# A two-layer decoder trunk on one core: the shift of each sublayer as two columns of the high activations, split once a layer, and another rule of waiting in the planner

## Chip, core and metric

The kernel runs on one core of a Trainium2 chip. The metric is device time in microseconds (us) of one execution; the lower the better. Before the change three runs took 947.19, 947.73 and 947.96 us, median 947.73. An execution under the profiler took 947.46 us. Its trace spans 945.7 us from the first to the last instruction, at a mean granted TensorE clock of 0.998.

## What is computed

A trunk of two layers, 256 tokens of width 1024, all in float32. Each layer has three sublayers: a SwiGLU feed-forward network (FFN), a token mixer (stick-breaking attention in layer 0, a gated linear recurrence in layer 1) and a second FFN. A conditioning vector `c` gives each sublayer a shift, a scale and a gate:

```python
mod = (c_act @ mod_w[layer] + mod_b[layer]).reshape(B, N_SUB, 3, D_MODEL)
...
h = rmsnorm(x, g) * (1 + scale[:, None, :]) + shift[:, None, :]
...
x = x + MACARON_W * g * swiglu(h, ffn_w_gu[layer, 0], ffn_w_down[layer, 0])
...
x = x + g * y
...
return rmsnorm(x, final_norm_g)
```

`D_FF` is 2816, the recurrent width 1280, and the weights fill some 249 MB, each read once.

## The kernel before

**Layout.** Activations are held transposed: `x` is eight tiles, one for each 128 of the 1024 features, of 128 partitions by 256 tokens. Weights stand still in TensorE, 128 x 128 at a time, and 256 token columns move through. A line number L610 is line 610 of the kernel.

**Three passes.** A float32 product is made of three float32r products. A number is split into a high part, rounded to float32r, and a low part, the rest. `group` (L598) issues for each piece of weights: high weights by high activations, high weights by low activations, low weights by high activations (`seq`, L607; the pass numbers are 0, 1, 2). Weights are split as they come in (`load`, L559): ACT copies the high part (`wh`, L581), DVE subtracts (`wl`, L584).

**A border** is the change from one sublayer to the next; five of the six sublayers have one ahead of them (generations (0,1), (0,2), (1,0), (1,1), (1,2)). The norm's factor for a token isn't known until all eight tiles of `x` are done, so the first two weight tiles behind a border (`NFIRST`) are computed from the activations without it. `scaled` (L712) makes for each chunk `d` a tile `hi` and a tile `lo` out of the ring `hx`, each of 258 columns (`TX`): 256 with `x` times the scale, and two with the shift, split anew for each chunk (L719, L720), the same value in both. `up_first` (L839) multiplies these 258 columns in all three passes, 2 weight tiles by 2 halves by 8 chunks. Its `evict` (L854) takes from PSUM the 256 columns times the factor `q` (tile `tr`, L857) and the product of the shift column (tile `bc`, L856). Meanwhile `norm` (L741) makes the normed activations, in `norm_chunk` (L725), for every weight tile that follows, with 256 columns.

**The rest of a sublayer.** `up` (L824) multiplies the normed `hx` by the weight tiles. `down` (L756) multiplies the result, which lies split in a high and a low half in the arena (`arenar`), by the down weights: for an FFN 22 chunks by 8 outputs by 3 passes, 528 matmuls; for the recurrent block 10 x 8 x 3, 240; for attention 8 x 8 x 3, 192. `residual` (L775) adds to `x` and calls `scaled` for the next border.

**Modulation.** Between the weight tiles, `mod_tile` (L636) computes shift, scale and gate of later sublayers on DVE from rows of `mod_w`, and `mod_final` (L648) adds the bias; for a shift (`w == 0`) that is L657.

**Places in SBUF.** Tiles get their addresses in the order of allocation, each rounded up to 32 bytes; the arena comes behind all of them. Three pads of odd sizes stand between: `HXPAD` 112, `HKPAD` 16 and `ARPAD` 56 columns of 4 bytes. With them the byte addresses in a partition are: `wh` from 43136, `wl` from 72704 (their views begin 0 or 128 bytes in, in turn, so that each begins at 128 modulo 256), `hx` from 102720 in steps of 1280, `hk` at 128384 and 129408, the arena at 168000. `hk` (L746, `other_copy`) holds a second copy of the first normed chunk; it is used for the first six matmuls of some weight tiles (`kick` in `up`), hx for the others. In a few places `kick_op` (L833) puts a short matmul of zeros ahead.

**The order of work** is planned by the program as it is built. `schedule` (L190) lists every operation with a cost, a due time (`prio`, from the TensorE order) and its dependences, and simulates the engines. For ACT and DVE, `wait_for` (L252) decides whether an operation that could start at `t` is held back because one that is due earlier will be ready at `g`, before the first would end; then a shorter one is taken or the engine idles. SP issues the weight loads in the planned order.

Of the kernel before, what the change touches and what calls it, by code (L numbers as in the profile page):

```python
# [8 lines left out]
F32R = mybir.dt.float32r  # L9
BF16 = mybir.dt.bfloat16  # L10
AF = mybir.ActivationFunctionType
ALU = mybir.AluOpType
PSUM = bass.MemoryType.PSUM

P = 128
T = 256
TX = T + 2
D = 1024
KD = D // P
# [111 lines left out]
class Program:  # L131
# [58 lines left out]
    def schedule(self):  # L190
# [23 lines left out]
        for o in reversed(ops):  # L214
            p = o.nominal if o.nominal is not None else self.pe + 1e5
            for s, data in o.succ:
                p = min(p, s.prio - o.cost - self.lag(o, s, data))
            for s, held in o.soft:
                p = min(p, s.prio - (o.cost + 100.0 if held else 0.0))
# [32 lines left out]
        def wait_for(e, t, o):  # L252

            q = queue[e]
            while head[e] < len(q) and q[head[e]].start is not None:
                head[e] += 1
            n, i = 0, head[e]
            slack = o.prio + late - t
            while n < LOOK and i < len(q):
                u = q[i]  # L260
                i += 1
                if u.start is not None:
                    continue
                n += 1
                if u is o or u.prio >= o.prio:
                    break
                g = guess(u, 3)
                if g is None or g >= t + o.cost or g <= t:
                    continue
                if u.prio + late - g < o.cost and u.prio + late - g < slack - MARGIN:  # L270
                    return g
            return None
# [17 lines left out]
        while len(order) < len(ops):  # L290
            best, again = None, False
            for e, c in cand.items():
                ok = []
                for o in c:
                    t = possible(o)
# [6 lines left out]
                for t, o in ok:  # L302
                    if t > t0:
                        continue
                    p = o.prio
# [4 lines left out]
                if e in queue:  # L310
                    g = wait_for(e, pick[2], pick[3])
# [15 lines left out]
            t, _, o = best  # L327
            cand[o.eng].remove(o)
            if o.eng == "ACT":
                if t - busy >= TABLE_NS and (gap is None or t - busy > gap[0]):  # L330
                    gap = (t - busy, o)
                if o.table is not None:
                    if o.table != table:
                        if gap is None:
                            t, gap = busy + TABLE_NS, (0.0, o)
# [15 lines left out]
            for b in o.bufs:  # L351
                b.uses -= 1
                if b.uses == 0 and b.space is not None:
# [3 lines left out]
                    t = o.end + 120.0 if b.hist else o.end  # L357
# [38 lines left out]
def c_dve(n):  # L396
    return 68.0 + 1.042 * n
# [11 lines left out]
def trunk(ctx, tc, first_in, cb, par, modw, gu, wdn, qk, wv, wo, win, wri, wout, out):  # L409
    at_ = {}  # L410
    for *key, n in first_order():
        o = sum(P * q.shape[1] for q in at_.values())
        at_[tuple(key)] = first_in[o : o + P * n].rearrange("(p n) -> p n", n=n)
    nc = tc.nc
    act, dve, pe, pool, sp = nc.scalar, nc.vector, nc.tensor, nc.gpsimd, nc.sync
    ctx.enter_context(tc.manual_schedule())
    pr = Program()
# [4 lines left out]
    def f32(ap):  # L422
        return ap.bitcast(F32)
# [74 lines left out]
    def fixed(name, cols, dt=F32):  # L498
        return const.tile([P, cols], dt, tag=name, name=name)
# [27 lines left out]
    mraw, mfin = {}, {}  # L527
# [5 lines left out]
    def col(off, n=1):  # L533
        return pars()[:, off : off + n]

    for l in range(2):
        for q in range(3):
            for w in range(3):
                mraw[l, q, w] = Buf(ap=fixed(f"mr{l}{q}{w}", KD))
                mfin[l, q, w] = Buf(ap=fixed(f"mf{l}{q}{w}", KD))  # L540
    gbias = Buf(ap=fixed("gbias", KD))
    fixed("pad1", ARPAD)


# [6 lines left out]
    def A(o, i, f, n, r, w, table=None, psum=False, ptr=0, after=(), **kw):  # L551
        def fn():
            act.activation(o(), i(), f, **{k: (v() if callable(v) else v) for k, v in kw.items()})  # L553
        return pr.op("ACT", c_act(n, psum, ptr), fn, r, w, after, table)

    def V(fn, n, r, w, cost=None, ptr=0):
        return pr.op("DVE", cost or c_dve(n) + 62.0 * ptr, fn, r, w)

    def load(src, n, name, chain=None, sizes=None, plain=0, homes=(), behind=(), kind=Buf):  # L559

# [30 lines left out]
    class Acc:  # L591
# [3 lines left out]
            self.b = Buf(banks, name=name)  # L595
            self.started = False

        def group(self, part, o, w, wc, xs, xc, stop, parts=(None,), passes=(0, 1, 2)):  # L598

            b = self.b  # L600
            start = not self.started
            self.started = True
            wh, wl = w
            xh, xl = xs

            def fn():
                seq = ((wh, xh), (wh, xl), (wl, xh))  # L607
                for n, i in enumerate(passes):
                    u, v = seq[i]
                    pe.matmul(o(b()), wc(u()), xc(v()), start=start and n == 0, stop=stop and n == len(passes) - 1,  # L610
                              skip_group_check=True)

            n = xs_n[0]
            ws = [wh] * (passes != (2,)) + [wl] * (2 in passes)
            rd = ws + [(t, q) for t in [xh] * (passes != (1,)) + [xl] * (1 in passes) for q in parts]
            if not start:
                rd.append((b, "start"))
            wr = [(b, part)] + ([(b, "start")] if start else [])
            return pr.op("PE", c_mm(n, len(passes)), fn, rd, wr)
# [8 lines left out]
        pr.op("PE", c_mm(n, 4), lambda: pe.matmul(o(b()), wc(w()), xc(x32()), start=start, stop=stop, skip_group_check=True),  # L628
              [w, x32] + ([] if start else [(b, "start")]), [(b, part)] + ([(b, "start")] if start else []))

    def group(acc, part, o, w, wc, xs, xc, n, stop, parts=(None,), passes=(0, 1, 2)):
        xs_n[0] = n
        return acc.group(part, o, w, wc, xs, xc, stop, parts, passes)


    def mod_tile(l, s, w, t, after=(), lat=None, rate=RATE, home=None, behind=()):  # L636
# [11 lines left out]
    def mod_final(l, s, w, t0=0, n=KD):  # L648
        m, f = mraw[l, s, w], mfin[l, s, w]
        b = OFF_MB + (l * 9 + s * 3 + w) * KD + t0  # L650
        rr = [(m, t) for t in range(t0, t0 + n)]
        ww = [(f, t) for t in range(t0, t0 + n)]
        pp = [(pars, 0)] if l == s == 0 else [pars]
        mi = lambda: m()[:, t0 : t0 + n]
        fo = lambda: f()[:, t0 : t0 + n]
        if w == 0:
            V(lambda: dve.tensor_tensor(fo(), mi(), col(b, n), ALU.add), n, rr + pp, ww)  # L657
            return
        V(lambda: dve.tensor_tensor(mi(), mi(), col(b, n), ALU.add), n, rr + pp, rr)
        if w == 1:  # L660
            g = OFF_NG + (l * 3 + s) * KD + t0
            V(lambda: dve.scalar_tensor_tensor(fo(), mi(), 1.0, col(g, n), ALU.add, ALU.mult), n, rr + pp, ww)
        else:
            wt = MAC if s != 1 else 1.0
            V(lambda: dve.tensor_scalar(fo(), mi(), 1.0, wt, ALU.add, ALU.mult), n, rr, ww)


    ssq, hcur, gcur, hkick = {}, {}, {}, {}

    def add_square(gen, d):  # L670
        if d == 0:
# [39 lines left out]

    def scaled(gen, d):  # L712

        gs, sh = mfin[gen + (1,)], mfin[gen + (0,)]
        hi, lo = Buf(hxr), Buf(hxr)
        gcur.setdefault(gen, []).append((hi, lo))
        c = slice(d, d + 1)
        shc = lambda: sh()[:, c].to_broadcast([P, 2])
        A(lambda: hi()[:, T:], shc, AF.Copy, 2, [(sh, d)], [(hi, 1)])  # L719
        V(lambda: dve.tensor_tensor(lo()[:, T:], shc(), f32(hi()[:, T:]), ALU.subtract), 2, [(sh, d), (hi, 1)], [(lo, 1)])  # L720
        A(lambda: hi()[:, :T], x[d], AF.Copy, T, [x[d], (gs, d)], [(hi, 0)], ptr=1, scale=lambda: gs()[:, c])
        V(lambda: dve.scalar_tensor_tensor(lo()[:, :T], x[d](), gs()[:, c], f32(hi()[:, :T]), ALU.mult, ALU.subtract), T,
          [x[d], (gs, d), (hi, 0)], [(lo, 0)], ptr=1)

    def norm_chunk(gen, d, q, whole=False):  # L725
        gs, sh = mfin[gen + (1,)], mfin[gen + (0,)]
        hp, hi, lo = Buf(hpr), Buf(hxr), Buf(hxr)
        hcur.setdefault(gen, []).append((hi, lo))
        c = slice(d, d + 1)
        V(lambda: dve.scalar_tensor_tensor(hp(), x[d](), gs()[:, c], q(), ALU.mult, ALU.mult), T,  # L730
          [x[d], (gs, d), q] + [(sh, d)] * whole, [hp], ptr=1)
        h = None
        if whole:
            h = Buf(hpr)
            V(lambda: dve.tensor_scalar(h(), hp(), sh()[:, c], None, ALU.add), T, [hp, (sh, d)], [h], ptr=1)
        A(lambda: hi()[:, :T], hp, AF.Identity, T, [hp, (sh, d)], [hi], ptr=1, bias=lambda: sh()[:, c])
        V(lambda: dve.scalar_tensor_tensor(lo()[:, :T], hp(), sh()[:, c], f32(hi()[:, :T]), ALU.add, ALU.subtract), T,
          [hp, (sh, d), hi], [lo], ptr=1)
        return h

    def norm(gen, q):  # L741
# [97 lines left out]
    def up_first(gen, ws, scale=(1.0, 1.0)):  # L839


        gx = gcur.pop(gen)
        accs = {}
        for i, w in enumerate(ws):
            accs[i] = [Acc(f"first_{gen}_{i}_{g}") for g in range(2)]
            for k in range(KD):
                if (i, k) == ((0, 6) if gen == (0, 1) else (1, 0)):
                    q = rstd(gen)
                for g in range(2):
                    c0 = (k % 4) * 256 + g * P  # L850
                    group(accs[i][g], 0, lambda b: b[:, :TX], w[k // 4], lambda u, c0=c0: u[:, c0 : c0 + P], gx[k],
                          lambda v: v, TX, k == KD - 1, parts=(0, 1))

        def evict(i, g):  # L854
            b, t, c = accs[i][g].b, Buf(tr), Buf(bcr)
            V(lambda: dve.tensor_scalar(c()[:, :1], b()[:, T : T + 1], scale[g], None, ALU.mult), 1, [b], [c])  # L856
            V(lambda: dve.scalar_tensor_tensor(t(), b()[:, :T], scale[g], q(), ALU.mult, ALU.mult), T, [b, q], [t])  # L857
            return t, c, lambda: c()[:, :1]

        norm(gen, q)  # L860
        for i in range(len(ws)):
            yield [evict(i, g) for g in range(2)]
# [693 lines left out]
```

## Time and profile before

| | |
|---|---|
| runs, median (lowest to highest) | 947.73 us (947.19 to 947.96) |
| the profiled execution | 947.46 us |
| its span | 945.7 us |
| TensorE matmuls (PE), weight loads (PEld) | 8078 of each |
| VectorE (DVE) instructions | 1279 |
| ScalarE (ACT) instructions | 914 |
| read from HBM | 248.92 MB, 264 GB/s over the span |

How to read the profile's rows: a row of the timeline or of the chain begins with the start and the length in us. In a row of groups stand line, engine, operation, out<-in by the program's tile names, partitions x elements and type, the count behind `x`, then the busy time in us and the mean duration of one in ns, then the engine's idle time before them. Matmuls overlap, so the mean duration of one isn't the spacing; that comes from the starts. A row of windows gives the stretch, its length, and then for PE, PEld, DVE, ACT (and POOL) the busy us and the count.

### The profile page before, as it was taken

Reading aid. Unit: us, or ns where it says so; the run is one execution under the profiler, and the core shown is the slowest. Engines: PE = TensorE matmul, PEld = TensorE weight load, DVE = VectorE, ACT = ScalarE, POOL = GpSimd, SP = SyncE. Lnnn points to the kernel's source line nnn. Section 1 sums busy time; section 2 is a strip of 40 time slices with the busy share of each in tenths; the row PEclk is TensorE's granted clock in tenths of the full one; section 3 lists DMA queues with packets and bytes.
Section 4 is the critical chain, followed back from the end, with each engine's and each line's share of the span. In section 5 each row is a group of like instructions: output and inputs, shape, how many; then the busy total and the mean of one; then the engine's idle time right before and its main releaser. Section 6 shows DMA issues by size and latency. Waiting matters only on the chain.

```text
span 945.7 us, 19610 instructions
## 1 busy us (share of the span) xinstructions
PE 934.8 (99%) x8078; PEld 924.2 (98%) x8078; DVE 781.6 (83%) x1279; ACT 559.3 (59%) x914; POOL 2.1 (0%) x14
## 2 busy tenths in 40 slices
PE   8999999999999999999999999999999999999996
PEld 6999999999999999999999999999999999999996
DVE  7999888899987989888799998866999997555443
ACT  5785553488785754454367554544789675554343
POOL 0000000000000000000000000000000000000000
PEclk9999999999999999999999999999999999999999
DMA  9989989948833699889967999885253646555421
GB/s 362 404 332 368 340 333 361 364 170 320 294 133 130 269 337 359 319 313 359 348 250 275 346 348 353 327 321 223 90 198 116 223 189 244 192 186 211 170 104 45
DMA packets 48332, 251.25 MB, mean 266 GB/s; under 512 B 5361, under 2 KB 5745, under 8 KB 28530
## 3 DMA queue, kind: packets, MB, share of 16 engines
q1 hardware_dynamic: 47952, 249.59, 70.2%
q8 instruction: 63, 1.03, 0.4%
q10 hardware_dynamic: 290, 0.40, 0.1%
q14 instruction: 27, 0.22, 0.1%
HBM read 248.92 MB, written 1.05 MB: 264 GB/s over the span
## 4 chain that ended last, share of the span: by engine, by line
PE 97%; DVE 2%; DMA 1%; ACT 0%; issue 0%; SPq 0%; DVEq 0%
PE bank L610 90%; PE bank L1041 2%; PE bank L1274 1%; PE bank L916 1%; DMA arenar<-in_first_in 1%; PE bank L1107 1%; PE bank L1168 1%; DVE wl L584 1%; PE bank L1144 1%; DVE arenar L644 0%; DVE x L1386 0%; PE bank L1147 0%; DVE arenaf L1358 0%; PE bank L703 0%; DVE arenaf L1345 0%
## 5 line engine op out<-in xcount | busy, mean ns | idle before, releaser
L610 PE MATMUL bank<-hx,wh 128*128 128x256 f32 (+1 forms) x3264 | 560.4, 277 | 0.0
L581 ACT ACTIVATE wh<-raw 128x1024 fp32r<-128x1024 f32 (+1 forms) x330 | 335.3, 1037 | 281.9 <-PE bank L610 199.0
L610 PEld LDWEIGHTS bank<-hx,wh 128*128 128x128 f32 x3264 | 492.7, 188 | 0.0
L584 DVE TENSOR_TENSOR wl<-raw,wh 128x1024 fp32r<-128x1024 f32 (+1 forms) x330 | 386.6, 1196 | 118.5 <-ACT wh L581 114.8
L610 PE MATMUL bank<-hx,wl 128*128 128x256 f32 (+1 forms) x1640 | 452.7, 277 | 0.0
L610 PEld LDWEIGHTS bank<-hx,wl 128*128 128x128 f32 x1640 | 308.4, 188 | 0.0
L610 PE MATMUL bank<-arenar,wh 128*128 128x256 f32 x1696 | 289.4, 276 | 0.0
L610 PEld LDWEIGHTS bank<-arenar,wh 128*128 128x128 f32 x1696 | 255.4, 188 | 0.2 <-issue 0.2
L610 PE MATMUL bank<-arenar,wl 128*128 128x256 f32 x848 | 234.3, 276 | 0.1
L644 DVE SCALAR_TENSOR_TENSOR rawm<-rawm,cact 128x1024 f32<-128x1024 f32 x128 | 154.7, 1220 | 8.2 <-DMA rawm<-in_modw 8.2
L610 PEld LDWEIGHTS bank<-arenar,wl 128*128 128x128 f32 x848 | 159.2, 188 | 0.3 <-DVE wl L584 0.3
L553 ACT ACTIVATE arenar<-a 128x256 fp32r<-128x256 f32 x88 | 35.3, 405 | 12.6 <-DVE a L869 10.8
L874 DVE TENSOR_TENSOR arenar<-a,arenar 128x256 fp32r<-128x256 f32 x88 | 36.4, 419 | 0.5 <-ACT arenar L553 0.5
L553 ACT ACTIVATE sg<-bank 128x256 f32<-128x256 f32 x82 | 30.0, 369 | 8.3 <-PE bank L610 8.1
L869 DVE TENSOR_TENSOR a<-bank,sg 128x256 f32<-128x256 f32 x82 | 34.1, 418 | 0.7 <-ACT sg L553 0.4
L553 ACT ACTIVATE arenaf<-bank 128x256 f32<-128x256 f32 (+1 forms) x53 | 23.2, 488 | 11.2 <-PE bank L610 5.1
L784 DVE SCALAR_TENSOR_TENSOR x<-bank,mf,x 128x256 f32<-128x256 f32 (+1 forms) x49 | 21.7, 473 | 9.2 <-PE bank L610 9.1
L553 ACT ACTIVATE hx<-x,mf 128x256 fp32r<-128x256 f32 x40 | 19.2, 500 | 16.3 <-DVE x L784 16.3
L553 ACT ACTIVATE hx<-hpre,mf 128x256 fp32r<-128x256 f32 x41 | 20.0, 504 | 11.4 <-DVE hpre L730 10.8
L1041 PE MATMUL bank<-wh,hx 128*128 128x256 f32 x128 | 23.0, 279 | 0.0
L644 DVE SCALAR_TENSOR_TENSOR arenar<-arenar,cact 128x1024 f32<-128x1024 f32 x16 | 19.5, 1221 | 1.9 <-DMA arenar<-in_first_in 1.9
L1496 ACT ACT_TABLE_LOAD x15 | 19.2, 1283 | 1.6 <-PEq L1544 1.3
(124 smaller groups left out, 504.2 us busy)
## 6 DMA issues: line engine op xcount, KB each, us to landing
raw<-in_gu SPq DMA_DIRECT2D x79, 1024.0 KB, 5.5
rawm<-in_modw SPq DMA_DIRECT2D x128, 512.0 KB, 6.9
raw<-in_wdn SPq DMA_DIRECT2D x44, 1024.0 KB, 4.9
raw<-in_win SPq DMA_DIRECT2D x10, 1024.0 KB, 4.9
arenar<-in_first_in SPq DMA_DIRECT2D x16, 512.0 KB, 7.8
raw<-in_qk SPq DMA_DIRECT2D x8, 1024.0 KB, 4.9
raw<-in_wout SPq DMA_DIRECT2D x5, 1024.0 KB, 4.8
raw<-in_first_in SPq DMA_DIRECT2D x8, 512.0 KB, 8.9
```

What stands on the lines that cost most here:

```text
L553: act.activation(o(), i(), f, **{k: (v() if callable(v) else v) for k, v in kw.items()})
L581: act.activation(h()[:, :m], raw()[:, a : a + m], AF.Copy)
L584: dve.tensor_tensor(lo()[:, :m], raw()[:, a : a + m], f32(h()[:, :m]), ALU.subtract)
L610: pe.matmul(o(b()), wc(u()), xc(v()), start=start and n == 0, stop=stop and n == len(passes) - 1, skip_group_check=True)
L644: dve.scalar_tensor_tensor(raw(), raw(), 1.0, cact(), ALU.mult, ALU.mult, accum_out=m()[:, t : t + 1])
L784: dve.scalar_tensor_tensor(x[d]()[:, w], acc.b()[:, j * T + w.start : j * T + w.stop], gate()[:, d : d + 1], x[d]()[:, w], ALU.mult, ALU.add)
L869: V(lambda: dve.tensor_tensor(a(), b()[:, T:], sg(), ALU.mult), T, [(b, (1, 0)), sg], [a])
L874: V(lambda: dve.tensor_tensor(y[1](), a(), f32(y[0]()), ALU.subtract), n, [a, y[0]], [y[1]])
L916: pr.op("PE", c_mm(T, 4), lambda: pe.matmul(b()[:, g * T : (g + 1) * T], raw()[:, c0 : c0 + P], h0(), start=start, stop=False, skip_group_ ...
L1041: pe.matmul(o, u()[:, tb * P : (tb + 1) * P], v()[:, c0 : c0 + 256], start=start and n == 0, stop=k == KD - 1 and n == 2, skip_group_check ...
L1107: pe.matmul(zb[e][i]()[:, j * m : (j + 1) * m], y()[rows, kc], y()[rows, qc], start=j == 0, stop=j == 1, skip_group_check=True)
L1496: act.preload_act_table_set(TABLES[t])
```

## The change

The shift is split once for each border, behind `mod_final`: ACT writes its high parts to the even columns of a new tile `shr` of 16 columns, DVE the low parts to the odd ones. `scaled` copies both, as two columns, into the high tile; the low tile's last two columns are no longer written. `group` gets a width `m` for the pass of the low activations, 256 columns in place of 258, and reads only the first part of the low tile. `evict` adds the two columns of the product. Both of its operations, and so the tiles `tr` and `bc`, now follow the last low activation of `norm` (`lows`). The five new tiles are allocated ahead of the last pad, which keeps its size: the arena begins 320 bytes later, at 168320.

In the planner, an operation is no longer held back where the idle time that this costs (`g - t`) is longer than the delay that it saves the other one (`t + o.cost - g`).

```diff
-                if g is None or g >= t + o.cost or g <= t:
+                if g is None or g >= t + o.cost or g <= t or t + o.cost - g < g - t:
                     continue
...
     gbias = Buf(ap=fixed("gbias", KD))
+    shr = {(l, q): Buf(ap=fixed(f"sh{l}{q}", 2 * KD, F32R)) for l in range(2) for q in range(3) if l or q}
     fixed("pad1", ARPAD)
...
-    def V(fn, n, r, w, cost=None, ptr=0):
-        return pr.op("DVE", cost or c_dve(n) + 62.0 * ptr, fn, r, w)
+    def V(fn, n, r, w, cost=None, ptr=0, after=()):
+        return pr.op("DVE", cost or c_dve(n) + 62.0 * ptr, fn, r, w, after)
...
-        def group(self, part, o, w, wc, xs, xc, stop, parts=(None,), passes=(0, 1, 2)):
+        def group(self, part, o, w, wc, xs, xc, stop, parts=(None,), passes=(0, 1, 2), m=None):
...
-                    pe.matmul(o(b()), wc(u()), xc(v()), start=start and n == 0, stop=stop and n == len(passes) - 1,
-                              skip_group_check=True)
+                    c = slice(0, m if i == 1 else None)
+                    pe.matmul(o(b())[:, c], wc(u()), xc(v())[:, c], start=start and n == 0,
+                              stop=stop and n == len(passes) - 1, skip_group_check=True)
...
-            rd = ws + [(t, q) for t in [xh] * (passes != (1,)) + [xl] * (1 in passes) for q in parts]
+            rd = ws + [(xh, q) for q in parts if passes != (1,)] + [(xl, q) for q in parts[:1] if 1 in passes]
...
             V(lambda: dve.tensor_tensor(fo(), mi(), col(b, n), ALU.add), n, rr + pp, ww)
+            if (l, s) in shr:
+                y = shr[l, s]
+                two = lambda i: y().rearrange("p (d i) -> p d i", i=2)[:, :, i]
+                A(lambda: two(0), fo, AF.Copy, KD, ww, [(y, 0)])
+                V(lambda: dve.tensor_tensor(two(1), fo(), f32(two(0)), ALU.subtract), KD, ww + [(y, 0)], [(y, 1)])
             return
...
-        gs, sh = mfin[gen + (1,)], mfin[gen + (0,)]
+        gs, y = mfin[gen + (1,)], shr[gen]
...
-        shc = lambda: sh()[:, c].to_broadcast([P, 2])
-        A(lambda: hi()[:, T:], shc, AF.Copy, 2, [(sh, d)], [(hi, 1)])
-        V(lambda: dve.tensor_tensor(lo()[:, T:], shc(), f32(hi()[:, T:]), ALU.subtract), 2, [(sh, d), (hi, 1)], [(lo, 1)])
+        A(lambda: hi()[:, T:], lambda: f32(y()[:, 2 * d : 2 * d + 2]), AF.Copy, 2, [(y, 0), (y, 1)], [(hi, 1)])
...
           [hp, (sh, d), hi], [lo], ptr=1)
+        lows[gen] = pr.ops[-1]
...
-                          lambda v: v, TX, k == KD - 1, parts=(0, 1))
+                          lambda v: v, TX, k == KD - 1, parts=(0, 1), m=T)
...
-            V(lambda: dve.tensor_scalar(c()[:, :1], b()[:, T : T + 1], scale[g], None, ALU.mult), 1, [b], [c])
-            V(lambda: dve.scalar_tensor_tensor(t(), b()[:, :T], scale[g], q(), ALU.mult, ALU.mult), T, [b, q], [t])
+            V(lambda: dve.tensor_scalar(c()[:, :1], b()[:, T : T + 1], b()[:, T + 1 : TX], scale[g], ALU.add, ALU.mult), 1, [b], [c],
+              ptr=1, after=[lows[gen]])
+            V(lambda: dve.scalar_tensor_tensor(t(), b()[:, :T], scale[g], q(), ALU.mult, ALU.mult), T, [b, q], [t],
+              after=[lows[gen]])
```

More of the change, by code (lines that the diff above doesn't have):

```diff
@@ L629, in group32, with group @@
               [w, x32] + ([] if start else [(b, "start")]), [(b, part)] + ([(b, "start")] if start else []))
-    def group(acc, part, o, w, wc, xs, xc, n, stop, parts=(None,), passes=(0, 1, 2)):
+    def group(acc, part, o, w, wc, xs, xc, n, stop, parts=(None,), passes=(0, 1, 2), m=None):
         xs_n[0] = n
-        return acc.group(part, o, w, wc, xs, xc, stop, parts, passes)
+        return acc.group(part, o, w, wc, xs, xc, stop, parts, passes, m)
     def mod_tile(l, s, w, t, after=(), lat=None, rate=RATE, home=None, behind=()):
@@ L665, in mod_final @@
             V(lambda: dve.tensor_scalar(fo(), mi(), 1.0, wt, ALU.add, ALU.mult), n, rr, ww)
-    ssq, hcur, gcur, hkick = {}, {}, {}, {}
+    ssq, hcur, gcur, hkick, lows = {}, {}, {}, {}, {}
     def add_square(gen, d):
```

## The prediction

> **What bounds the kernel.** I read the page first, then the chain of waits, the groups by shape, and last the timeline of TensorE around the borders.
>
> ```profile
> span 945.7 us, 19610 instructions
> PE 934.8 (99%) x8078; PEld 924.2 (98%) x8078; DVE 781.6 (83%) x1279; ACT 559.3 (59%) x914; POOL 2.1 (0%) x14
> PE 97%; DVE 2%; DMA 1%; ACT 0%; issue 0%; SPq 0%; DVEq 0%
> ```
>
> TensorE is busy for 99% of the span and is 97% of the chain. So the time is a count of matmuls times their spacing, and an edit on another engine counts only where it makes TensorE wait. What remains is the spacing, which a mean duration hides because neighbours overlap; I take it from start to start. Three stretches of the timeline:
>
> ```profile
> 314.35 0.40 PE L610 MATMUL bank<-hx,wh 128*128 128x258 f32 x2
> 314.59 0.28 PE L610 MATMUL bank<-hx,wl 128*128 128x258 f32 x1
> 314.71 0.41 PE L610 MATMUL bank<-hx,wh 128*128 128x258 f32 x2
> ...
> 315.07 0.40 PE L610 MATMUL bank<-hk,wh 128*128 128x256 f32 x2
> ...
> 315.79 0.40 PE L610 MATMUL bank<-hx,wh 128*128 128x256 f32 x2
> ...
> 316.49 0.39 PE L610 MATMUL bank<-hx,wh 128*128 128x256 f32 x2
> ...
> 318.53 0.39 PE L610 MATMUL bank<-hx,wh 128*128 128x256 f32 x2
> ```
>
> ```profile
> 678.21 0.39 PE L610 MATMUL bank<-hk,wh 128*128 128x256 f32 x2
> 678.44 0.28 PE L610 MATMUL bank<-hk,wl 128*128 128x256 f32 x1
> ...
> 678.91 0.40 PE L610 MATMUL bank<-hx,wh 128*128 128x256 f32 x2
> 679.27 0.39 PE L610 MATMUL bank<-hx,wh 128*128 128x256 f32 x2
> ```
>
> ```profile
> 744.30 0.39 PE L610 MATMUL bank<-arenar,wh 128*128 128x256 f32 x2
> ...
> 746.00 0.39 PE L610 MATMUL bank<-arenar,wh 128*128 128x256 f32 x2
> ...
> 746.34 0.39 PE L610 MATMUL bank<-arenar,wh 128*128 128x256 f32 x2
> 746.84 0.38 PE L610 MATMUL bank<-arenar,wl 128*128 128x256 f32 x1
> ```
>
> One shape, 256 columns, has several spacings. hx at 316.49 to 318.53: 18 matmuls in 2.04 us, 113.3 ns. The arena at 744.30 to 746.00: 15 in 1.70, also 113.3. hk at 315.07: six in 0.72, 120 ns, entered from the slow 258-column stretch; at 678.21, entered from a fast one, six in 0.70, 117 ns, and fast again at 679.27, three matmuls after it is left. The 258-column ones: 314.35 to 314.71, three in 0.36, some 120 ns, though two columns more are 0.9 ns by proportion. Two more views, the chain in order of time and busy time by windows for the arena's instructions alone (its columns end with the clock, the DMA share and GB/s), show the slow pace lasting with 256 columns:
>
> ```profile
> 281.70 8.48 PE bank L610 x72
> ...
> 746.84 15.37 PE bank L610 x130
> ```
>
> ```profile
> 281.60:289.80 8.20, 8.20 (x72) 8.20 (x72) 0.69 (x1) 0.63 (x1) 1.00 0.52 188
> ...
> 424.00:483.70 59.70, 59.70 (x528) 59.70 (x528) 0.53 (x2) 0.42 (x1) 1.00 0.93 352
> 729.40:746.40 17.00, 17.00 (x152) 17.00 (x152) 2.74 (x4) 2.50 (x4) 1.00 0.43 146
> ```
>
> The stretch at 281.70 in the chain has 8.48 us for 72, 117.8 ns; a down projection (424.00 in the windows of arena instructions) 59.70 for 528, 113. The clock column is 1.00 in both. So the pace has a memory: a run keeps the fast or the slow step it came in with.
>
> What sets hk apart from hx is only its place. By the program's addresses, modulo 256 bytes, every weight view starts at 128, hx at 64, the arena at 64, and hk at 128. Moving data 64 bytes behind the weights can hold 113.3; moving data level with the weights (hk) was slow in all of its short runs.
>
> **The change, part by part.** *The arena moves.* Five shr tiles of 16 columns, 64 bytes each, are allocated ahead of pad1, whose 56 columns stay. The arena goes from 168000 to 168320, which is 128 modulo 256: level with the weights, like hk (384 modulo 512 and modulo 1024 too). All down projections read their moving operand there.
>
> ```profile
> L610 PE MATMUL bank<-arenar,wh 128*128 128x256 f32 x1696 | 289.4, 276 | 0.0
> L610 PE MATMUL bank<-arenar,wl 128*128 128x256 f32 x848 | 234.3, 276 | 0.1
> ```
>
> That is 2544: four FFNs of 528, 240 in the recurrent block, 192 in attention, of which 18 + 72 are slow already. Fast now: 2454. This state in a long run the trace doesn't show, so I bound its price per matmul: 0 if it falls into the fast step, 117.8 - 113.3 = 4.5 ns by the stretch at 281.70, 120 - 113.3 = 6.7 ns by hk from a slow entry. I take 119, between hk's two entries (117 and 120) and nearer the later matmuls of both: 5.7 ns x 2454 = +14.0 us (0, 11.0 and 16.4 at the bounds). Nothing hides it, since TensorE doesn't wait in these stretches. The Trainium skill speaks against this term: SBUF — State Buffer, section "Who interferes with whom", gives TensorE two independent read ports, for the moving operand and for weight loads, and says that PE never waits on anyone; by it the term would be 0 and the time 947.2 us. The trace disagrees: 113.3, 117.8 and 120 ns for one shape at one clock.
>
> *Low activations of 256 columns.* One pass in three at each border: 2 tiles x 2 halves x 8 chunks x 5 borders = 160.
>
> ```profile
> L610 PE MATMUL bank<-hx,wh 128*128 128x258 f32 x288 | 52.5, 284 | 0.0
> L610 PE MATMUL bank<-hx,wl 128*128 128x258 f32 x152 | 43.1, 284 | 0.0
> L610 PE MATMUL bank<-hx,arenar 128*128 128x258 f32 x40 | 5.8, 284 | 0.0
> L553 ACT ACTIVATE hx<-mf 128x2 fp32r<-128x2 f32 x40 | 5.9, 197 | 2.8 <-DVE mf L657 2.8
> L720 DVE TENSOR_TENSOR hx<-mf,hx 128x2 fp32r<-128x2 f32 x40 | 4.6, 154 | 1.3 <-ACT hx L553 1.2
> L659 DVE TENSOR_TENSOR mr<-mr,x 128x8 f32<-128x8 f32 x11 | 1.8, 163 | 0.1
> L856 DVE TENSOR_SCALAR bc<-bank 128x1 f32<-128x1 f32 x20 | 2.4, 151 | 0.0
> ```
>
> Between 258-column neighbours these should keep the slow step: 120 to 118 ns, -0.3 us. Bounds: 0.9 ns each, -0.1; all 480 of the border falling to 114, -2.9.
>
> *Shift split once.* 40 two-element DVE subtractions (154 ns) go; 5 of eight elements come (some 163 ns by the nearest row), with 5 ACT copies of some 200 ns. ACT's 40 copies into hx stay. The 20 evictions to bc read a second scalar from PSUM. DVE is rid of 6.2 - 0.8 = 5.4 us. TensorE's matmuls hide DVE at the borders, and a gain can't be more than TensorE's idle time, 0.4 us below; I take 0. The split puts an ACT and a DVE step, under 1 us together, between the shift and the first copy into hx:
>
> ```profile
> L657 DVE TENSOR_TENSOR mf<-mr,x x5: 158/167/170, 154.1 to 600.2; 128x8 f32<-128x8 f32 x5
> ```
>
> ```profile
> 197.69 0.24 PE bank L695 x2
> ```
>
> The first of the five shifts is ready at 154.1, the sum of squares of its border runs at 197.69: 0. Were a shift late, its border would wait that 1 us.
>
> *Evictions behind the last low activation.* On DVE they queue behind the sixteen chunk operations, and behind them wait ACT's silu and the bank's release. TensorE has the next tile's eight chunks meanwhile, and those come sooner. 0; if the cover went, one stall like that at 746.34.
>
> *The planner* idles less on ACT and DVE, so both orders change everywhere. What it can win is TensorE's idle time behind the start: the two matmuls from 746.34 take 0.50 instead of 0.23 and the next 0.22 instead of 0.11, 0.4 us in all. What it can lose is an operation put ahead of a due one, a weight split of 1.2 us, where DVE has no room:
>
> ```profile
> 730.00:746.00 16.00, 16.00 (x143) 16.00 (x142) 15.93 (x21) 11.87 (x18) 0.00 (x0) 1.00 0.43 144
> ```
>
> DVE is busy 15.93 of 16 us ahead of that stall. I take 0, bounds -0.4 and +1.2 us.
>
> **Sum.** The profiled execution took 947.46 us, 0.27 under the median and inside the runs' spread. 947.46 + 14.0 - 0.3 = 961.2; I say 961. Bounds of this case: +11.0 - 2.9 - 0.4 gives 955.2, +16.4 - 0.1 + 1.2 gives 965.0.
>
> **Rivals.** *The level arena falls into the fast step (not slower).* hk's runs are six matmuls; an FFN's down is 528. If the step is found from the seventh matmul on, as hx finds it three behind hk, the 14 us vanish and 947.46 - 0.3 = 947.2 is left, 944.6 if the borders go fast as well (2.9). For it: 678.21 begins with two matmuls in 0.23. Against it: after them no hk run speeds up, and the stretch at 281.70 shows that 72 matmuls need not find it. The skill's rule on ports, above, ends at the same time.
>
> *Some of the runs go slow.* The FFNs enter from fast hx, the recurrent block behind a kick, attention from its sums. With two of the four FFNs slow: 1056 x 5.7 = 6.0 us, 953.2. For it: two steps at one address exist. Against: FFN entries are alike.
>
> *DVE becomes the bound at 730 to 747.* A weight split late by 1.2 us stops TensorE at the last down: 948.4 without the arena's cost, no more than the measurement tells. For it 15.93 of 16; against it the 5 us that DVE is rid of.
>
> **Chances.** About 0.2%, 1.9 us, is what a measurement tells from no change. All downs slow, 72% (955.2 to 965.0). Some slow, 7%, 949.5 to 955. Fast arena, 18%: 12% within 0.2%, 6% faster by over 0.2% (under 945.8), if the borders go fast too. DVE alone, 3%, 1% of it beyond 0.2%. Slower 72 + 7 + 1 = 80%, same 14%, faster 6%. The likeliest's own range is 955 to 965; 72% isn't enough, so it reaches down to 947, over the partial case and half of the fast arena's.
>
> **What would show it.** In the chain, a down projection of 528 at 62 to 63 us instead of 59.8, its timeline at 0.35 to 0.36 us per three, hx groups still 0.34. Border tiles near 0.36 per three. Wrong if the arena keeps 0.34, or if PE's waits grow by microseconds at the borders or at the last down.

## The result, and the profile after

| | median, us | lowest to highest | ratio to the kernel before, 95% interval |
|---|---|---|---|
| before, 5 runs | 947.96 | 947.19 to 949.27 | |
| changed, 5 runs | 975.33 | 974.76 to 975.81 | 1.0287 (1.0272 to 1.0302) |

The change makes the kernel 2.9% slower, 27 us; forecast were 961 us, and at most 965. The profiled execution of the changed kernel took 975.81 us. Its page answers to the first lines shown of before:

```profile
span 973.7 us, 19585 instructions
PE 963.8 (99%) x8078; PEld 953.1 (98%) x8078; DVE 782.6 (80%) x1244; ACT 558.2 (57%) x919; POOL 2.1 (0%) x14
PE 99%; DVE 0%; DMA 0%; ACT 0%; DVEq 0%; issue 0%; ACTq 0%
L612 PE MATMUL bank<-arenar,wh 128*128 128x256 f32 x1696 | 305.8, 283 | 0.0
```

TensorE executes the same 8078 matmuls, is again busy for 99% of the span and is now 99% of the chain. None of its waits grew; the matmuls have become longer (a mean of 283 ns for the arena's, 276 before). Where that happens is read from the chain in order of time, which cuts the run at each border's sum of squares. (L610 has become L612.) First before, then after:

```profile
35.63 162.06 PE bank L610 x1426
...
309.44 180.28 PE bank L610 x1584
...
489.96 180.28 PE bank L610 x1584
...
762.45 174.49 PE bank L610 x1536
```

```profile
36.01 165.50 PE bank L612 x1426
...
314.06 187.85 PE bank L612 x1584
...
502.15 187.84 PE bank L612 x1584
...
690.22 16.67 PE bank L612 x144
...
748.70 34.23 PE bank L612 x285
...
783.17 182.13 PE bank L612 x1536
```

The three stretches of an FFN behind a border lose 7.6 us each (187.85 - 180.28), 22.8 of the 28.0 us of span. The first FFN loses 3.4. A down projection alone, in the view by windows of the arena's instructions:

```profile
134.00:197.00 63.00, 63.00 (x527) 63.00 (x526) 0.42 (x1) 0.42 (x1) 1.00 0.90 338
433.00:495.90 62.90, 62.90 (x526) 62.90 (x525) 0.42 (x1) 0.42 (x1) 1.00 0.87 329
```

The second row holds 526 matmuls, those cut at its edges included, in 62.9 us at a clock of 1.00; by the starts it is 120.0 ns, 113.3 before: 528 x 6.7 = 3.5 us. That is the first FFN's loss, and was forecast. The other 4.1 us of each later FFN lie ahead of its down. The timeline of TensorE at the end of the border (0,2), the place that the prediction shows from 314.35 to 318.53 before:

```profile
318.89 0.40 PE L612 MATMUL bank<-hx,wh 128*128 128x258 f32 x2
319.13 0.28 PE L612 MATMUL bank<-hx,wl 128*128 128x258 f32 x1
319.24 0.41 PE L612 MATMUL bank<-hx,wh 128*128 128x258 f32 x2
319.49 0.28 PE L612 MATMUL bank<-hx,wl 128*128 128x258 f32 x1
319.61 0.40 PE L612 MATMUL bank<-hk,wh 128*128 128x256 f32 x2
...
320.31 0.40 PE L612 MATMUL bank<-hx,wh 128*128 128x256 f32 x2
...
321.38 0.40 PE L612 MATMUL bank<-hx,wh 128*128 128x256 f32 x2
...
323.85 0.40 PE L612 MATMUL bank<-hx,wh 128*128 128x256 f32 x2
```

hx at 321.38 to 323.85: 21 matmuls in 2.47 us, 117.6 ns, where there were 113.3. (A row merges passes 0 and 1, so it names the first one's 258 columns alone.) Over the 954 hx matmuls of a stretch the starts in the trace give a mean of 117.8 ns in (0,2), (1,0) and (1,2): 954 x 4.5 = 4.3 us. In (1,1) hx is back at 113.4. So hk's six matmuls, behind which hx was fast at all four borders before, no longer make it so at three of the four.

### The profile page after: what moved, and what is told of

The parts are those of the page before. It is cut to its first block, busy times and chain, and to the rows that moved or that the text cites. A ratio compares the mean times of both kernels' runs of the same rounds, so it can differ in the third digit from the quotient of the medians.

```text
span 973.7 us, 19585 instructions
## 1 busy us (share of the span) xinstructions
PE 963.8 (99%) x8078; PEld 953.1 (98%) x8078; DVE 782.6 (80%) x1244; ACT 558.2 (57%) x919; POOL 2.1 (0%) x14
## 4 chain that ended last, share of the span: by engine, by line
PE 99%; DVE 0%; DMA 0%; ACT 0%; DVEq 0%; issue 0%; ACTq 0%
PE bank L612 92%; PE bank L1049 2%; PE bank L1282 1%; PE bank L924 1%; PE bank L1115 1%; PE bank L1176 1%; PE bank L1152 1%; PE bank L710 0%; PE bank L1429 0%; DMA rawm<-in_cb 0%; DVE x L1394 0%; PE bank L1155 0%; PE bank L702 0%; ACT rms L554 0%; ACT rst L554 0%; DVEq L1559 0%
## 5 line engine op out<-in xcount | busy, mean ns | idle before, releaser
L612 PE MATMUL bank<-hx,wh 128*128 128x256 f32 (+1 forms) x3264 | 572.4, 280 | 0.0
L612 PEld LDWEIGHTS bank<-hx,wh 128*128 128x128 f32 x3264 | 496.6, 188 | 0.0
L612 PE MATMUL bank<-hx,wl 128*128 128x256 f32 (+1 forms) x1640 | 457.2, 280 | 0.0
L612 PEld LDWEIGHTS bank<-hx,wl 128*128 128x128 f32 x1640 | 312.2, 190 | 0.0
L612 PE MATMUL bank<-arenar,wh 128*128 128x256 f32 x1696 | 305.8, 283 | 0.0
L612 PEld LDWEIGHTS bank<-arenar,wh 128*128 128x128 f32 x1696 | 264.5, 192 | 0.2 <-issue 0.2
L612 PE MATMUL bank<-arenar,wl 128*128 128x256 f32 x848 | 240.0, 283 | 0.0
L612 PEld LDWEIGHTS bank<-arenar,wl 128*128 128x128 f32 x848 | 162.8, 192 | 0.0
L1049 PEld LDWEIGHTS bank<-wh,hx 128*128 128x128 f32 x128 | 19.9, 188 | 0.1
```

The costliest lines, as they stand in the source:

```text
L612: pe.matmul(o(b())[:, c], wc(u()), xc(v())[:, c], start=start and n == 0, stop=stop and n == len(passes) - 1, skip_group_check=True)
L1049: pe.matmul(o, u()[:, tb * P : (tb + 1) * P], v()[:, c0 : c0 + 256], start=start and n == 0, stop=k == KD - 1 and n == 2, skip_group_check ...
```

## The experiments

**Which part does it.** The first theory gave the arena's place and the narrower low pass a price each.

```diff
-HXPAD, HKPAD, ARPAD = 112, 16, 56
+HXPAD, HKPAD, ARPAD = 112, 16, 136
```

> The kernel before with one edit: the last pad grows by 80 columns, so that the arena begins at 168320, as after the change; all instructions are the same. Theory P (place and width have a price each): the arena's matmuls go from 113.3 to 120.0 ns, 2454 x 6.7 = +16.4 us, the normed hx tiles stay at 113.3: some 964 us. Rival E (entry): the slow arena alone also hands its step through the border to hx, then three FFNs' 954 hx matmuls at 117.8 come on top, +12.9: some 977 us. Rival N (planner): 948 us.

Measured: 964.0 us, ratio 1.0169 (1.0154 to 1.0184). Its chain has, for the stretch of 180.28 us:

```profile
313.20 183.82 PE bank L610 x1584
```

That is 3.54 us more, the arena's 528 x 6.7, and hx stays at 113.4 ns. An address alone, with no instruction changed, costs 1.7%. The Trainium skill (SBUF — State Buffer, section "Who interferes with whom") has TensorE wait on nobody, its moving operand and its weight loads on ports of their own; read as a rule for the spacing too, that would make e1 as fast as the kernel before, and the run disagrees.

Next, the changed kernel with the arena put back, `ARPAD` 40 in place of 56:

> The changed kernel with the last pad cut from 56 to 40 columns, so that the arena begins at 168256, again 64 bytes behind the weights modulo 256; the order of work is that of the changed kernel. Theory P: the arena is fast again, the border of 258, 256, 258 columns still leaves three FFNs' hx in the slow step: 947.9 + 12.9 - 0.8 = 960 us. Rival E: with the arena all is fast again: 947 us. Rival N: 975 us.

Measured: 947.49 us, ratio 0.9997 (0.9987 to 1.0006), the stretch as follows, and hx at 113.4.

```profile
310.28 180.10 PE bank L612 x1584
```

This falls on rival E's figure, but only by chance, since e1 had already refuted E; and it refutes theory P: the low pass has no 12.9 us of its own. The low pass by itself, in the kernel before:

```diff
-                          lambda v: v, TX, k == KD - 1, parts=(0, 1))
+                          lambda v: v, TX, k == KD - 1, parts=(0, 1), m=T)
```

(with `group` taking `m` as in the change)

> The kernel before with the pass of the low activations at the borders cut from 258 to 256 columns and nothing else; it leaves out the product of the high weights with the low part of the shift. Theory P: the border gains some 0.8 us, and the hx matmuls of three FFNs keep the slow step, 3 x 954 x 4.5 = +12.9: some 960 us. Rivals E and N: 947 us, or a few tenths less.

Measured: 946.45 us, ratio 0.9984 (0.9975 to 0.9993); the stretch is 180.10 us again. Against 180.28 that is 0.18 us for the 96 border matmuls in it, 1.9 ns each; by the starts they go from 120.7 to 118.9 ns. And the planner's rule by itself:

```diff
-                if g is None or g >= t + o.cost or g <= t:
+                if g is None or g >= t + o.cost or g <= t or t + o.cost - g < g - t:
```

> The kernel before with the planner's new rule and nothing else. Theory P and rival E: no more than 0.5 us either way, 947.5 to 948.5 us. Rival N: 12 us and more, 960 us or over.

Measured: 947.45 us, ratio 0.9997 (0.9988 to 1.0007): nothing. So neither part alone slows hx. That left the two together:

> The kernel before with the arena at 168320 (as in e1) and the low pass of 256 columns (as in e3), and nothing else of the change; it leaves out the product of the high weights with the low part of the shift. Theory J (the two together make what neither makes alone: a border of 258, 256, 258 columns entered from the slow arena ends in a step that hk does not turn): arena +16.4, three times 954 hx matmuls at 117.8 instead of 113.3 for +12.9, borders -0.8: some 976 us. Rival S (the two prices only add, and the slow hx comes from the split, the order behind the last low activation or the planner): 964.0 - 1.7 = 962 us.

Measured: 975.18 us, ratio 1.0288 (1.0271 to 1.0305), the whole loss of the change out of a pad and a slice:

```profile
313.40 187.85 PE bank L611 x1584
```

| median, us | low pass of 258 | low pass of 256 |
|---|---|---|
| arena at 64 modulo 256 | 948.2 (before) | 946.5 (e3) |
| arena at 128 | 964.0 (e1) | 975.2 (e5) |

The prices don't add: 16 and -2 would give 962. Theory J stands; its claim that only the step of hx is wrong was tested next.

**Is hx in a wrong step, or slowed by something that lasts?** The changed kernel with a jolt, a short matmul, behind the first three hx matmuls of the first tile of `up`:

```diff
                       lambda u, c0=c0: u[:, c0 : c0 + P], h, lambda v: v[:, :T], T, k == KD - 1)
+                if kick and gen in ((0, 2), (1, 0), (1, 2)) and (k, g) == (1, 0):
+                    kick_op(acc, 0, (0, 0))
```

> The changed kernel, with a matmul of 64 columns of zeros (kick_op) behind the second chunk of the first tile of `up`, in the three FFNs whose hx matmuls stayed at 117.8 ns. Theory J: only the step is wrong, and a jolt turns it as in the first FFN: 975.3 - 12.9 + 0.3 = 963 us. Rival M (the hx matmuls are slowed by something that lasts, such as the work of the other engines): 975 us.

Measured: 963.5 us, ratio 1.0165 (1.0150 to 1.0180). Its timeline at the jolt:

```profile
321.59 0.40 PE L612 MATMUL bank<-hx,wh 128*128 128x256 f32 x2
321.83 0.28 PE L612 MATMUL bank<-hx,wl 128*128 128x256 f32 x1
321.95 0.20 PE L844 MATMUL bank<-ident,zero 128*128 128x64 bf16 x1
321.99 0.48 PE L612 MATMUL bank<-hx,wh 128*128 128x256 f32 x2
322.31 0.28 PE L612 MATMUL bank<-hx,wl 128*128 128x256 f32 x1
322.43 0.39 PE L612 MATMUL bank<-hx,wh 128*128 128x256 f32 x2
...
323.79 0.39 PE L612 MATMUL bank<-hx,wh 128*128 128x256 f32 x2
```

From 322.43 to 323.79 twelve matmuls take 1.36 us, 113.3 ns, and the 951 behind the jolt keep that pace (a mean of 113.4). Three matmuls of 64 columns, one for each FFN, give back 12 us, the arena being as slow as before. hx was in a step that nothing else keeps up; rival M falls.

**What makes the step.** Lists of the single starts, taken from the traces, show that a border of 258, 256, 258 columns goes by two triples in turn. The last six matmuls of the border (0,2), then hk's six, then the first three of hx, each as ns to the next start:

```
changed kernel   116 119 118  120 122 119 | 118 118 120  117 117 118 | 119 119 117   then 117.8
e2, arena back   120 123 118  116 118 119 | 121 116 119  119 121 116 | 119 121 116   then 113.4
```

Whichever of the two triples comes last seems to decide what hk leaves. One more triple should then turn it, whatever the arena does:

```diff
+        if gen in ((0, 2), (1, 0), (1, 2)):
+            group(Acc("odd"), 0, lambda b: b[:, :TX], ws[-1][1], lambda u: u[:, 7 * P :], gx[-1], lambda v: v, TX, True,
+                  parts=(0, 1), m=T)
```

> The changed kernel with one group of three matmuls more (258, 256, 258 columns, the last chunk once more, into a bank that nobody reads) at the end of the border of the three FFNs. In the traces a border of the new widths goes by two alternating triples, about 120 122 119 and 116 118 118 ns; behind the one hk's six matmuls leave hx slow, behind the other fast. Theory B (the beat: which triple comes last decides): one triple more turns it, hx at 113.3, arena at 120.0: 975.3 - 12.9 + 3 x 0.36 = 963.5 us. Rival A (a border behind a slow arena leaves hx slow whatever its length): 976.4 us.

Measured: 963.19 us, ratio 1.0153 (1.0118 to 1.0188). Three matmuls more in each of three FFNs, 12 us less:

```profile
318.94 0.40 PE L612 MATMUL bank<-hk,wh 128*128 128x256 f32 x2
...
320.01 0.39 PE L612 MATMUL bank<-hx,wh 128*128 128x256 f32 x2
...
321.03 0.39 PE L612 MATMUL bank<-hx,wh 128*128 128x256 f32 x2
```

From 320.01 to 321.03 nine hx matmuls take 1.02 us, 113.3 ns, behind a slow arena. The same group where all was fast:

> The same extra group in the kernel of e2 (the arena back 64 bytes behind the weights, where hx was fast). Theory B: the triple that comes last is now the other one, and the three FFNs' hx matmuls fall to 117.8 ns with a fast arena: 947.5 + 12.9 + 1.1 = 961.5 us. Rival A: 947.5 + 1.1 = 948.6 us.

Measured: 963.27 us, ratio 1.0160 (1.0109 to 1.0211). Three rows of its windows, all instructions: hx of (0,2), the down behind it, hx of (1,2):

```profile
318.30:430.50 112.20, 112.20 (x955) 112.20 (x954) 96.94 (x153) 57.52 (x88) 0.00 (x0) 1.00 0.83 312
430.70:492.70 62.00, 62.00 (x529) 62.00 (x528) 50.53 (x76) 26.32 (x37) 0.00 (x0) 1.00 0.90 334
785.10:893.00 107.90, 107.90 (x954) 107.90 (x954) 69.75 (x100) 57.31 (x87) 0.00 (x0) 1.00 0.56 204
```

The arena is in its good place, and hx of (0,2) takes 112.2 us for its 954, 117.8 ns by the starts; (1,0) does the same. The down takes the slow step over: 62 us for 528, 117.8 ns by the starts, 2.4 us more. Two FFNs by 4.3 + 2.4, and 1.1 for the three extra groups, are 14.5 us; measured from e2's 947.5 are 15.8. In the profiled execution pauses of TensorE make the border (0,1) 2.0 us longer than in e2 (13.68 against 11.65).

In (1,2) the border came out on the fast triple in spite of the extra group, and hx there is fast. The starts show that the extra group did turn it: the triple ahead of the extra one is 120 122 118, the extra one 116 119 118. At all six borders with the extra group (e10, e11) it is the other triple than the one ahead of it. So this border's triples stood the other way round than in e2. The down ahead of it had changed its step: 113.3 ns up to a pause of TensorE at 762.1 us, 117.8 in the 82 matmuls behind it, where e2 goes on at 113.3 behind a like pause. The row of the chain behind the pause, those 82 and 48 of the border, has a counterpart before at 746.84:

```profile
762.55 15.63 PE bank L612 x130
```

Whether the changed step is what turned the border wasn't tested; (1,0), also entered at 117.8, stood as in e2. Nor is it shown why (1,1) of the changed kernel ends on the fast triple behind a slow arena.

Over the eight kernels with the new widths there are 32 borders that end in hk, 11 on the triple 120 122 119 and 21 on 116 118 119, each number within 1 ns. Behind the first hx went on at 117.8 in the eight cases where it was left alone; the other three are e6's, with the short matmul three matmuls on. Behind the second it went on at 113.3 to 113.5 in all 21, pauses of TensorE left out. Eight of these are (1,1), where only 12 or 42 hx matmuls follow.

**Other places for the arena.** The kernel before with the pad 32 and 48 columns longer, one run each:

> The kernel before with the last pad 32 columns longer: the arena begins at 168128, 192 modulo 256, that is 64 bytes ahead of the weights' place. No theory of mine fixes the price; if only the place 64 bytes behind the weights is fast, the arena's matmuls take 117 to 120 ns and the run some 959 to 964 us; if only the level place is slow, 948 us.

> The kernel before with the last pad 48 columns longer: the arena begins at 168192, 0 modulo 256, 128 bytes from the weights' place either way. As in the run before: 959 to 964 us if only the place 64 bytes behind the weights is fast, 948 us if only the level place is slow.

Measured: 956.38 and 960.03 us. A down projection of an FFN in each, by windows of the arena's instructions, and for the first place that of the recurrent block:

```profile
425.60:487.60 62.00, 62.00 (x528) 62.00 (x527) 0.48 (x2) 0.42 (x1) 1.00 0.90 337
735.20:762.50 27.30, 27.19 (x236) 27.00 (x236) 2.74 (x4) 2.51 (x4) 1.00 0.53 194
```

```profile
427.20:489.70 62.50, 62.50 (x528) 62.50 (x528) 0.54 (x2) 0.42 (x1) 1.00 0.90 336
```

The starts give 117.8 and 118.7 ns. In the first place the recurrent block's down, which begins behind a short matmul, runs at 113.3 up to a pause of TensorE at 752.6 us and at 117.8 in the 82 behind it: there both steps exist too. The downs of the four FFNs alone make 2112 x 4.5 = 9.5 us, and the run stays under the 959 us that were expected. Of the four places in steps of 64 bytes, only the one 64 bytes behind the weights is fast in the FFNs. e2 has the arena 256 bytes beyond the old place and is as fast: that fits a period of 256 bytes. The weights begin at 128 modulo 256 in every run, so whether it is the place against the weights that counts or the address alone isn't shown.

**A version that keeps the rest.** The changed kernel without the planner's rule and with `ARPAD` 40:

> The changed kernel without the planner's new rule and with the last pad cut to 40 columns, so that the arena is back 64 bytes behind the weights modulo 256. By theory J the arena and the hx matmuls are fast, and what is left of the change is the border: 480 matmuls 1.7 ns closer, -0.8 us, and less work on DVE: 946.5 to 947.2 us, 0.1 to 0.2% under the kernel before. If the shift's split or the order of the evictions had a price of its own, it would show here: 948 us or more.

Measured: 947.97 us, ratio 1.0016 (0.9999 to 1.0033), over the 946.5 to 947.2 that were expected; three of its twelve runs took 953 to 954 us, as one of seven of the kernel before did beside e10. No gain can be told from no change. In its trace the hx matmuls of (1,2), where the chain goes through DVE, have a mean of 114.4 ns, pauses included, against 113.4 in e2: 1.0 us, as much as the border saves. With the pad mended the changed kernel (e2) equals the one before, and only e3, which leaves a product out, is below it, by 0.07 to 0.25%.

## Why the prediction was wrong

*What bounds the kernel.* Right. The 28 us are matmul spacing; no wait of TensorE grew. One row I misread: the 130 matmuls from 746.84 are, by the starts, 82 of the arena at 113.3 and 48 of the border at 120.8, and show no slow pace that lasts. The 72 from 281.70 do, at 117.8.

*The arena moves: +14.0 us.* The mechanism was right and the size low. I took 119 ns, between hk's two entries; a long run is at 120.0, the upper bound, 6.7 x 2454 = 16.4. e1 alone measures 964.0 against 948.2. Two matmuls of hk near the fast pace at its entry, 0.23 us from 678.21, pulled my mean down; they belong to the change of step, not to the state.

*Low activations of 256 columns: -0.3 us.* This is the step that failed. I priced the 480 border matmuls and stopped at the border's end, and wrote that the hx groups would stay at 0.34 us per three. The border's own saving was there and larger, some 0.9 us (1.9 ns x 480, from e3's stretch). But the new widths alternate between two triples, and behind a slow arena three of four borders end on the one that hk doesn't turn; the hx matmuls behind them, priced at nothing, then run at 117.8 instead of 113.3: 3 x 954 x 4.5 = 12.9 us. The fact was in my text, "a run keeps the fast or the slow step it came in with", and the sum used it for the arena alone. e5 makes the loss, e6 and e10 take it away, e11 makes it with a fast arena.

The two together: 947.5 + 16.4 + 12.9 - 0.9 = 975.9, for 975.8 in the profiled execution.

*Shift split once, evictions, planner: 0 each.* Right to some 0.1%: together with the border's saving, and with the arena back, 0.9997 (e2). They may have cost the 0.9 us of that saving; the trace has a pause of TensorE of 0.8 us near 43.5 us, whose cause wasn't tested. The planner alone is 0.9997 (0.9988 to 1.0007, e4), so it wins or loses no more than some 0.1% by itself.

*Rivals.* The fast arena fell with e1, whose downs of 528 never find the fast step. Some of the runs slow fell too: all the FFNs' downs were slow. DVE as the bound fell: the changed kernel's chain goes through DVE only in the first 12 and the last 6 us. None of my rivals was about the matmuls behind the border, and so the range ended 10 us short.

## What to carry to other kernels

When an edit adds a tile, look at the addresses of everything allocated behind it: here 320 bytes cost 1.7% (e1), and a pad of the right size undoes it (e2). Price a matmul stretch not only by its own spacing but by the step in which it leaves the next one; where two edits touch the same step, measure them alone and together, since here +16 and -2 us made +27. Where a stretch of equal matmuls runs at 117.8 ns and a like one at 113.3, a single short matmul between them is a cheap test of whether only the step is wrong.

## What the runs showed of the hardware

The spacing of float32r matmuls of 256 columns depended on where the moving operand began modulo 256 bytes, with weights that begin at 128: in the downs of the FFNs 113.3 ns at 64 (before), 120.0 at 128 (e1), 117.8 at 192 (e7) and 118.7 at 0 (e8). The level place is thus not the only slow one. At 64 there are two steps, 113.3 and 117.8, and both lasted for 954 matmuls (hx in e2 and in the changed kernel). What was seen to change them: a border of other width, hk at another place, a short matmul (e6), and once a pause of TensorE (e11). At 192 both steps were seen as well (e7). At 128 a short matmul changed nothing: behind the one at the start of the recurrent block's down (row 748.70 of the chain after) the matmuls go on at 120.0. What in the chip makes the steps was not tried.
